# Two blocks in one kernel: the scale of the first norm made by matrix products, and a rope weight block whose rotated copy the host lays out

## The chip, the cores and the metric

The kernel runs on one core of one Trainium2 chip. The metric is the device time of one execution in microseconds; lower is better. TensorE (PE in the profile, PEld its weight loads), VectorE (DVE), ScalarE (ACT), GpSimd (POOL) and the DMA engines, whose work is issued by SyncE (SP), run side by side and wait for each other through semaphores.

## The reference

Two transformer blocks stand one after the other, each two layers deep, on 256 tokens of width 1024. Only the start of the first block is touched. Each layer makes six vectors from a condition `c` and scales and shifts a norm with two of them:

```
mod = silu(c) @ w_mod[l] + b_mod[l]                 # 1024 -> 6144
sh1, sc1, gt1, sh2, sc2, gt2 = split(mod, 6)
h = rms_norm(x, g_norm_mix[l]) * (1 + sc1) + sh1
proj = h @ w_in[l]                                  # 1024 -> 1952
q_d, k_d, v_d, cq, ckv, k_rope = split(proj)        # k_rope: the last 32 columns
```

`k_rope` is normed and rotated: with its two halves of 16 columns, rope gives (x1 cos - x2 sin, x2 cos + x1 sin). Two attentions (one dilated, one latent), an output product, a two-layer MLP and the residuals follow; then the second layer, and the second block (two other attentions, a dense MLP, a routed mixture of experts).

## The kernel before

All is float32. Each weight block of 1 MB (128 partitions x 2048 columns) is loaded into a tile `raw`, of which there are five (`NRAW`). ACT makes a rounded copy `whl` (hi), DVE the remainder (lo), and a product is three matmuls: hi by hi, hi by lo, lo by hi (`mm3`, `mtile`; a tile `mt` of 128 output rows takes 24 matmuls). The norm's factor over the tokens (`rstd`) is multiplied in after the product, when DVE takes a tile out of PSUM (`ev`); the scale over the features, `G = (1 + sc1) * g`, goes into `h_hi` and `h_lo` before it. So layer 0 can start no `mt` before `sc1` is there.

In layer 0 the scale comes from `mod_rows(0, ..., 8, 16, fine=14)`: PE spreads `silu(c)` over the partitions (`cb`), and for each of the eight groups of 128 outputs DVE multiplies a row block of the transposed weight by it and sums (`TENSOR_TENSOR_REDUCE`, in the profile CUSTOM_DVE_ANT_0 on `raw<-raw,cb`); the last 1 MB comes in two halves. The shift comes later and in another way, by `mod_part(0, 0, 8)`: per 1 MB block of the untransposed weight four matmuls of 512 columns (`mod<-raw,c_pad`), then a copy `mod_e` on DVE, four transposes `mod_t` on PE, a reduction and an addition on DVE. What the shift adds to the first four tiles (a bias for each output) is a small product `shb`; the later tiles have two more columns of h (256 to 258) that carry it.

The rope columns: for the rotation PE needs a tile of 64 columns, the 32 and the same with the halves exchanged. ACT and DVE make its hi and lo in three pieces each, out of a `raw` of 160 columns per k.

The order is not written by hand. Every instruction is recorded; `Sched` runs a list scheduler over the records with its own costs, and issues in the order that it finds. For each phase of the program the table `FINAL` gives a base order, three parameters of looking ahead, and the size and the seed of a noise on the priorities. `RESERVE` keeps buffers free for stretches of operation numbers. Every engine then runs its list strictly in that order. The whole of it is one source line, so the profile shows nearly all work at L641; tiles tell the work apart. The phase names are `start` (up to the rope tables), `first_mix0`, `first_mlp0`, and so on.

Of the kernel before, what the change touches and what calls it, by code (L numbers as in the profile page):

```python
# [159 lines left out]

class Op:
    __slots__ = ("i", "eng", "calls", "reads", "writes", "dur", "deps", "succ", "nd", "allocs", "start", "end", "prio",
                 "lat", "touch", "label", "phase", "after", "wait", "at", "hold", "goal")

    def __init__(self, eng):
        self.eng, self.calls, self.reads, self.writes, self.dur, self.lat = eng, [], [], [], 0.0, 0.0
# [19 lines left out]
class Sched:  # L186
# [2 lines left out]

    FINAL = {None: (1, (0.7, 0.2, 20), 0, 0),  # L190
             "start": (1, (0.3, 0.1, 10), 3, 377680),
             "first_mix0": (1, (0.6, 0.1, 30), 3, 220609),
             "first_mlp0": (1, (0.5, 0.1, 8), 8, 801976),
             "first_mix1": (1, (0.7, 0.3, 8), 15, 101696),
             "first_mlp1": (1, (0.5, 0.1, 30), 2, 868914),
             "second_mix0": (2, (0.6, 0.1, 20), 8, 40661),
# [1 line left out]
             "second_mix1": (1, (0.6, 0.1, 20), 10, 580917),  # L198
             "route": (2, (0.5, 0.1, 8), 0, 185731),
             "moe": (2, (0.3, 0.1, 10), 8, 572101)}  # L200
    RESERVE = {"t1": [(-73, 177)], "t2": [(247, 497), (1312, 1562), (2540, 2790), (2551, 2801), (3732, 3982), (3757, 4007), (3768, 4018), (3518, 4018), (1343, 1593), (3882, 4132)]}
    goal = None
    ISSUE = 1.22
    LATENCY = {("PE", "ACT"): 0.2, ("PE", "DVE"): 0.2, ("ACT", "PE"): 0.23, ("DVE", "PE"): 0.2, ("DVE", "ACT"): 0.13,
# [2 lines left out]
    def __init__(self, nc):  # L207
        self.nc = nc
        self.ops = []
        self.limits = {}  # L210
        self.group = None
        self.reserve = {}
        self.bufs = []
        self.bias = 0
        self.after = None
        self.phase = "start"
        self.gen = 0
        self.done_deps = -1
# [95 lines left out]
    def add(self, op):  # L314
        op.i = len(self.ops)
        op.phase = self.phase
        op.prio = op.i + self.bias
        op.after = self.after
        self.ops.append(op)
# [93 lines left out]
    def use(self, prios, plan):  # L413
        n = len(self.ops)
        noise = {}
        for op in self.ops:
            base, op.hold, amp, seed = plan.get(op.phase) or plan[None]
            op.prio = prios[base][op.i]
            if amp:
                if seed not in noise:  # L420
                    noise[seed] = np.random.RandomState(seed).rand(n)
                op.prio += amp * (noise[seed][op.i] - 0.5)

    def justify(self):

# [48 lines left out]
    def attempt(self):  # L474
# [23 lines left out]
        goal, last = self.goal, 0.0  # L498
# [14 lines left out]
        def can(op):  # L513
            need = {}
            op.allocs = [b for b in op.touch if id(b) not in allocated and b.ap is None]
            for b in op.allocs:
                k = (id(b.pool), b.tag)
                need[k] = need.get(k, 0) + 1
            for k, n in need.items():
                lim = self.limits[k]  # L520
                fr = lim - live[k]
                if fr < n:
                    self.short = k
                    return False

                p = pend[k]
                while ptr[k] < len(p) and id(p[ptr[k]]) in allocated:
                    ptr[k] += 1
                oldest = p[ptr[k]]
                if oldest in op.touch:  # L530
                    continue
                i = oldest.alloc_op.i
                r = self.LIMIT_RESERVE + sum(lo <= i <= hi for lo, hi in self.reserve.get(k, ()))
                if fr - n < max(min(r, lim - 1), lim == 1):
                    self.short = k
                    return False
            return True

        while left:
# [57 lines left out]
            if not ev:  # L597
                op = min((o for h in ready.values() for _, _, o in h), key=lambda o: o.i)
                assert not can(op)
                return self.short, op.i  # L600
            t = max(t, ev[0][0])
            while ev and ev[0][0] <= t + 1e-9:
                _, _, x = heapq.heappop(ev)
# [93 lines left out]
def small_arrays(I):  # L697
# [14 lines left out]
    for l in range(2):  # L712
# [22 lines left out]

BIG = ["w_kv_up", "w_router_2"]

PACKED = {"in_a": ("w_in", 0, 1024, 0, 1792, 8, 256), "in_b": ("w_in", 0, 1024, 1792, 160, 8, 160),
          "q_up": ("w_q_up", 0, 256, 0, 768, 2, 768), "out": ("w_out", 0, 1024, 0, 1024, 4, 512),
          "mlp_in": ("w_mlp_in", 0, 1024, 0, FF1, 8, 256), "mlp_out": ("w_mlp_out", 0, FF1, 0, 1024, 2, 1024),  # L740
          "mod": ("w_mod", 0, 1024, 0, 6144, 4, 512), "modT": ("w_modT", 0, 6144, 0, 1024, 2, 1024),
# [20 lines left out]
def body(ctx: ExitStack, tc: tile.TileContext, I, SN, out):  # L762
    nc = tc.nc
    S_ = Sched(nc)
# [395 lines left out]
    A.preload_act_table_set("natural_log_exp_and_others")  # L1160
    ca, cp = silu_c()
    mods = [tl("act", [128, 48], F32, f"mod{l}") for l in range(2)]
    mod_rows(0, c_rows("E4"), 8, 16, fine=14)

    trig = tl("cst", [128, 256], F32, "trig")
    trk = tl("cst", [64, 256], F32, "trk")
# [55 lines left out]
    def first_mix(l, acc, gt):  # L1222
# [55 lines left out]
        else:  # L1278
# [8 lines left out]
                        mm3(ps[j][:, :n], (w[0][:, k, sl], w[1][:, k, sl]), (h[kk][0][:, :n], h[kk][1][:, :n]), kk == 0, kk == 7)  # L1287
                        S_.end()
            ps.append(mtile(wsplit(rb[1][:, :, :128]), h))
        khl = hilo([128, 8, 64])  # L1290
        kr_src = rb[1][:, :, 128:160]
        for dsl, ssl in ((slice(0, 32), slice(0, 32)), (slice(32, 48), slice(16, 32)), (slice(48, 64), slice(0, 16))):
            split(kr_src[:, :, ssl], khl[0][:, :, dsl], khl[1][:, :, dsl])
        pr = mtile(khl, h, m=64, n=n)
        if l == 0:

            mod_part(0, 0, 8)
            shift_cols(h, shift(mods[0], 0))
            sp = t256("sh_pad").rearrange("p (k s) -> p k s", s=32)
            V.memset(sp, 0.0)  # L1300
            V.tensor_copy(sp[:, :, 0], mods[0][:, 0:8])
            pb = bank("shb")
            for hf in range(2):
                S_.begin()
                for o, r in ((0, rb[0]), (256, rb[1])):
                    for k in range(4):
                        T.matmul(pb[32 * k:32 * k + 32, o:o + r.shape[2]], sp[:, 4 * hf + k], r[:, 4 * hf + k],
                                 start=hf == 0 and o == 0, stop=hf == 1, skip_group_check=True)
                S_.end()
            e = t512("shb_e")  # L1310
            V.tensor_copy(e[:, :416], pb[:, :416])
            V.tensor_copy(e[:, 416:432], pb[:, 400:416])
            V.tensor_copy(e[:, 432:448], pb[:, 384:400])
            pt = bank("shb_t")
            S_.begin()
            for j in range(4):
                w = min(128, 448 - 128 * j)
                T.transpose(pt[:w, j * 128:(j + 1) * 128], e[:, j * 128:j * 128 + w], ident)
            S_.end()
            bc = tl("act", [128, 4], F32, "bc", "bc")  # L1320
            for m, c0, c1 in ((128, 0, 3), (64, 3, 4)):
                V.tensor_reduce(bc[:m, c0:c1], pt[:m, 128 * c0:128 * c1].rearrange("p (b r s) -> p b r s", r=4, s=32)[:, :, :, 0],
                                AX.X, OP.add)
            for j, pb in enumerate(ps + [pr]):
                early[id(pb)] = bc[:, j:j + 1]
            rope_tables()
            distances()
# [811 lines left out]
            run(S_.in_order)  # L2139


NRAW, NW, NT1, NR1, NT2 = 5, 6, 10, 7, 6
NAHEAD = 4
PM0 = 40
# [4 lines left out]
def host_arrays(I):  # L2149
# [5 lines left out]
    for n, (src, *how) in PACKED.items():  # L2155
        w = np.asarray(I["w_mod" if src == "w_modT" else src])
        w = w.transpose(0, 2, 1) if src == "w_modT" else w
        a[n] = pack(w.reshape(-1, *w.shape[-2:]), *how)
    gu = np.asarray(I["w_gu_exp_2"][0])
    g, u = gu[:, :, :FE], gu[:, :, FE:]  # L2160
    cols = [x[:, :, c:c + 256] for c in range(0, FE - 128, 256) for x in (g, u)] + [g[:, :, FE - 128:], u[:, :, FE - 128:]]
# [21 lines left out]
```

## Time and profile before

| what | value |
|---|---|
| time of the runs | 1593.61, 1597.28, 1599.37 us: median 1597.28 us |
| profiled execution | 1594.11 us, of which the span of the trace is 1592.3 us |
| PE busy | 1538.5 us, 97% of the span |
| DVE busy | 999.6 us, 63% |
| ACT busy | 797.7 us, 50% |
| moved by DMA | 384.35 MB, mean 241 GB/s |
| mean granted TensorE clock | 0.995 of full speed |

PE is busy nearly throughout, so what counts is the time in which it stands still or runs at half rate. The span is the time from the first to the last instruction; 1.81 us of the execution lie outside it.

### The profile page before, as it was taken

How to read it: one execution, taken by the hardware profiler on the slowest of the kernel's cores; microseconds unless marked ns; L12 is line 12 of the kernel's file. 1: busy time of each engine (PE TensorE's matmuls, PEld its weight loads, DVE VectorE, ACT ScalarE, POOL GpSimd, SP SyncE). 2: the span in 40 equal slices, each digit the busy share in tenths (PEclk: the TensorE clock that was granted, in tenths of full speed). 3: DMA queues.
4: the chain of work that ended last, by engine and by line, in shares of the span. 5: the costliest groups of instructions: out<-in, count | busy, mean ns of one | idle time of the engine just before them, and what ended most of it. 6: DMA issues, size and time to landing. Idle time of an engine off the chain costs nothing. (4 is left out here: it accounts for less than half of the span.)

```text
span 1592.3 us, 36673 instructions
## 1 busy us (share of the span) xinstructions
PE 1538.5 (97%) x15441; PEld 1356.7 (85%) x15441; DVE 999.6 (63%) x2117; ACT 797.7 (50%) x1519; POOL 9.9 (1%) x22
## 2 busy tenths in 40 slices
PE   5989999999999999999999999999999999998997
PEld 4777999998889999999999999999899755675564
DVE  7889898988998655788677666687856400000001
ACT  3857656567766655566865444466775200000000
POOL 0000000000000000010000000010000000000000
PEclk9999999999999999999999999999999999999999
DMA  9845598874146654554265555464337589999995
GB/s 350 314 183 212 203 358 334 331 279 171 42 159 223 227 189 159 185 186 137 91 225 180 191 202 195 163 212 143 123 117 307 210 354 414 418 417 392 418 418 220
DMA packets 59707, 384.35 MB, mean 241 GB/s; under 512 B 7936, under 2 KB 10640, under 8 KB 16912
## 3 DMA queue, kind: packets, MB, share of 16 engines
q1 hardware_dynamic: 57664, 379.78, 62.4%
q8 instruction: 125, 2.05, 0.5%
q0 software_dynamic: 832, 2.11, 0.5%
q14 instruction: 46, 0.38, 0.1%
q10 hardware_dynamic: 1040, 0.03, 0.0%
HBM read 380.83 MB, written 1.06 MB: 240 GB/s over the span
## 5 line engine op out<-in xcount | busy, mean ns | idle before, releaser
L641 PE MATMUL mt<-h_hi,whl 128*128 128x256 f32 (+2 forms) x3264 | 621.3, 285 | 11.4 <-ACT h_hi L641 11.4
L641 PEld LDWEIGHTS mt<-h_hi,whl 128*128 128x128 f32 (+1 forms) x3264 | 515.8, 189 | 25.6 <-ACT h_hi L641 11.9
L641 ACT ACTIVATE whl<-raw 128x1024 fp32r<-128x1024 f32 (+4 forms) x404 | 382.4, 960 | 282.3 <-PE mt L641 147.0
L641 DVE TENSOR_TENSOR whl<-raw,whl 128x1024 fp32r<-128x1024 f32 (+4 forms) x404 | 442.0, 1103 | 125.8 <-ACT whl L641 124.8
L641 PE MATMUL mt<-h_lo,whl 128*128 128x256 f32 (+2 forms) x1632 | 461.6, 283 | 1.0 <-DVE h_lo L641 1.0
L641 PEld LDWEIGHTS mt<-h_lo,whl 128*128 128x128 f32 (+1 forms) x1632 | 309.2, 189 | 1.6 <-DVE h_lo L641 1.4
L641 PE MATMUL acc<-a_hi,whl 128*128 128x256 f32 x1376 | 254.0, 280 | 0.0
L641 PEld LDWEIGHTS acc<-a_hi,whl 128*128 128x128 f32 x1376 | 216.4, 189 | 0.0
L641 PE MATMUL gu<-raw,xg 128*32 (+1 forms) x3520 | 201.8, 380 | 6.0 <-issue 6.0
L641 PE MATMUL acc<-a_lo,whl 128*128 128x256 f32 x688 | 192.6, 280 | 0.0
L641 PEld LDWEIGHTS gu<-raw,xg 128*32 128x32 f32 x3520 | 131.8, 110 | 70.4 <-issue 16.3
L641 DVE TENSOR_TENSOR sg<-sg,gu 128x512 f32<-128x512 f32 (+2 forms) x18 | 9.9, 561 | 205.0 <-PE gu L641 185.6
L641 PEld LDWEIGHTS acc<-a_lo,whl 128*128 128x128 f32 x688 | 129.3, 188 | 0.0
L641 PE MATMUL y<-raw,aT 128*32 (+1 forms) x1760 | 100.9, 384 | 4.9 <-DMA raw<-in_dn_e_dram 2.8
L641 DVE TENSOR_TENSOR ev<-mt,rstd 128x256 f32<-128x256 f32 (+1 forms) x166 | 69.4, 421 | 49.1 <-PE mt L641 48.5
L641 PEld LDWEIGHTS y<-raw,aT 128*32 128x32 f32 x1760 | 57.6, 111 | 43.9 <-issue 5.3
L641 DVE CUSTOM_DVE_ANT_0 raw<-raw,cb 128x1024 f32<-128x1024 f32 x64 | 76.9, 1221 | 5.4 <-ACT cb L641 3.0
L641 DVE SCALAR_TENSOR_TENSOR y_lo<-y,ws,y_hi 128x256 fp32r<-128x256 f32 x20 | 8.7, 480 | 100.3 <-ACT y_hi L641 100.3
L641 ACT ACTIVATE aT<-aT 128x256 f32<-128x256 f32 (+1 forms) x33 | 9.9, 346 | 104.1 <-PE aT L641 91.6
L641 ACT ACTIVATE y_hi<-y,ws 128x256 fp32r<-128x256 f32 x20 | 8.4, 471 | 105.8 <-issue 53.6
L641 ACT ACTIVATE sg<-gu 128x512 f32<-128x512 f32 (+2 forms) x18 | 8.7, 496 | 97.8 <-PE gu L641 97.8
L641 ACT ACTIVATE ev<-ev,bcol 128x256 f32<-128x256 f32 x64 | 32.0, 500 | 46.4 <-DVE bcol L641 31.4
(308 smaller groups left out, 1955.3 us busy)
## 6 DMA issues: line engine op xcount, KB each, us to landing
raw<-in_gu_e_dram SPq DMA_DIRECT2D x88, 1024.0 KB, 11.0
raw<-in_mlp_in_dram SPq DMA_DIRECT2D x32, 1024.0 KB, 5.1
raw<-in_mlp_out_dram SPq DMA_DIRECT2D x32, 1024.0 KB, 5.3
raw<-in_dn_e_dram SPq DMA_DIRECT2D x32, 1024.0 KB, 14.6
raw<-in_modT_dram SPq DMA_DIRECT2D x31, 1024.0 KB, 6.6
raw<-in_in_dram SPq DMA_DIRECT2D x24, 1024.0 KB, 4.8
raw<-in_gu_d_dram SPq DMA_DIRECT2D x22, 1024.0 KB, 4.9
raw<-in_mod_dram SPq DMA_DIRECT2D x16, 1024.0 KB, 7.1
```

The costliest lines, as they stand in the source:

```text
L641: getattr(real, m)(*[res(x) for x in a], **{k: res(x) for k, x in kw.items()})
```

## The change

Four things change.

1. `mod_rows(0, c_rows("E4"), 8, 16, fine=14)` becomes `mod_part(0, 8, 16)`: the scale is made as the shift is. The eight VectorE multiply-and-sum instructions and the spreading product `cb` go; 16 matmuls of 512 columns, a copy, four transposes, two reductions and the addition come. The weight is the untransposed one, in four blocks of 1 MB instead of three and two halves.
2. The host lays the block `in_b` out with 192 columns per k: 160 as before, then the two halves of the rope columns exchanged. The kernel splits columns 128 to 192 in one piece (one ACT, one DVE instruction, in each layer), and the copies of `shb_e` become one.
3. The noise is drawn by a number `ni` that is the operation's number plus a constant (`SH`), so that later phases draw what they drew before.
4. `FINAL` has other entries for `first_mix0` and `first_mlp0`, and `RESERVE` for `t2` is another list.

```diff
-                 "lat", "touch", "label", "phase", "after", "wait", "at", "hold", "goal")
+                 "lat", "ni", "touch", "label", "phase", "after", "wait", "at", "hold", "goal")
...
-             "first_mix0": (1, (0.6, 0.1, 30), 3, 220609),
-             "first_mlp0": (1, (0.5, 0.1, 8), 8, 801976),
+             "first_mix0": (1, (0.6, 0.1, 30), 3, 564062),
+             "first_mlp0": (2, (0.7, 0.3, 20), 1, 768677),
...
-        self.bias = 0
+        self.bias = self.shift = 0
...
+        op.ni = op.i + self.shift
...
-                    noise[seed] = np.random.RandomState(seed).rand(n)
-                op.prio += amp * (noise[seed][op.i] - 0.5)
+                    noise[seed] = np.random.RandomState(seed).rand(n + 1000)
+                op.prio += amp * (noise[seed][op.ni] - 0.5)
...
-    mod_rows(0, c_rows("E4"), 8, 16, fine=14)
+    mod_part(0, 8, 16)
...
-        khl = hilo([128, 8, 64])
-        kr_src = rb[1][:, :, 128:160]
-        for dsl, ssl in ((slice(0, 32), slice(0, 32)), (slice(32, 48), slice(16, 32)), (slice(48, 64), slice(0, 16))):
-            split(kr_src[:, :, ssl], khl[0][:, :, dsl], khl[1][:, :, dsl])
-        pr = mtile(khl, h, m=64, n=n)
+        pr = mtile(wsplit(rb[1][:, :, 128:192]), h, m=64, n=n)
+        S_.shift = SH[l]
...
-            V.tensor_copy(e[:, :416], pb[:, :416])
-            V.tensor_copy(e[:, 416:432], pb[:, 400:416])
-            V.tensor_copy(e[:, 432:448], pb[:, 384:400])
+            V.tensor_copy(e[:, :448], pb[:, :448])
...
+SH = (25, 29)
...
+    w = np.asarray(I["w_in"])
+    w = w[:, :, [*range(1792, 1952), *range(1936, 1952), *range(1920, 1936)]]
+    a["in_b"] = pack(w, 0, 1024, 0, 192, 8, 192)
```

The lists of the engines show what this moves. First VectorE, from the condition to the first of the norm's remainders `h_lo`. Before, where the ISA rows are the multiply-and-sum and the reading of its sum, and eight such pairs stand:

```order
L641 COPY c_pad<-c_act 128x8
L641 ISA raw,mod_140<-raw,cb 128x1024
L641 ISA mod_140 128x1
...
L641 TENSOR_TENSOR whl<-raw,whl 128x512
L641 TENSOR_TENSOR mod_140<-mod_140,SM 128x8
L641 SCALAR_TENSOR_TENSOR G_167<-mod_140,SM 128x8
L641 TENSOR_TENSOR whl<-raw,whl 128x512
L641 SCALAR_TENSOR_TENSOR h_lo<-x,G_167,h_hi 128x256 x6
```

And the same stretch of VectorE's list in the changed kernel:

```order
L642 COPY c_pad<-c_act 128x8
L642 COPY mod_e<-mod 128x512
L642 TENSOR_TENSOR whl<-raw,whl 128x512
L642 TENSOR_REDUCE mod_152<-mod_t 128x4 x2
L642 TENSOR_TENSOR whl<-raw,whl 128x512
L642 TENSOR_TENSOR mod_152<-mod_152,SM 128x8
L642 SCALAR_TENSOR_TENSOR G_161<-mod_152,SM 128x8
L642 TENSOR_REDUCE sqr<-sqs 128x256
L642 SCALAR_TENSOR_TENSOR h_lo<-x,G_161,h_hi 128x256 x5
```

Between the product and `G` two weight remainders `whl` now stand, where one stood, and behind `G` the sum of squares `sqr` has moved ahead of all `h_lo`. On ACT the square `sqs` of the first half of x and a third `whl` likewise stand ahead of the first `h_hi` now. On PE the product `ssq` over `sqr` stands ahead of the first `mt`; before, the 48 matmuls of the first two `mt` tiles stood ahead of it.

Second PE, around the last block of the shift's product and the rope tile (`mt` of 64 rows, 24 matmuls). Before:

```order
L641 MATMUL mt<-h_hi,whl 64x256
L641 MATMUL mod<-raw,c_pad 32x512 x4
L641 MATMUL mod_t<-K,mod_e 128x128 x4
L641 MATMUL shb<-raw,sh_pad 32x256 x4
L641 MATMUL shb<-raw,sh_pad 32x160 x4
...
L641 MATMUL mt<-h_hi,whl 128x258
```

And PE's list at this place in the changed kernel, where half of the rope tile stands behind the product:

```order
L642 MATMUL mod<-raw,c_pad 32x512 x4
L642 MATMUL mt<-h_hi,whl 64x256
L642 MATMUL mt<-h_lo,whl 64x256
...
L642 MATMUL mt<-h_hi,whl 64x256
L642 MATMUL mod_t<-K,mod_e 128x128 x4
L642 MATMUL shb<-raw,sh_pad 32x256 x4
L642 MATMUL shb<-raw,sh_pad 32x192 x4
```

The transposes `mod_t`, which need VectorE's copy `mod_e`, stood right behind the product; now 12 matmuls of the rope tile stand between.

Third VectorE, in the attention of layer 0, where the latent query's tiles (`qm`) are multiplied (`qm_g`) and the keys are scaled (`km`). Before:

```order
L641 SCALAR_TENSOR_TENSOR rn_hl<-rn_hi,K,rs_r 128x256
L641 TENSOR_TENSOR whl<-raw,whl 128x1024
L641 TENSOR_TENSOR ev<-mt,rstd 128x256
L641 TENSOR_TENSOR km<-rnb,kn_g 64x256 x2
L641 TENSOR_TENSOR whl<-raw,whl 128x1024 x2
L641 TENSOR_TENSOR qm_g<-qm,trq 128x512
L641 COPY bcol<-mt 128x1
L641 TENSOR_TENSOR km<-rnb,kn_g 64x256 x3
```

And VectorE's list in the changed kernel, where its first `qm_g` stands:

```order
L642 SCALAR_TENSOR_TENSOR rn_hl<-rn_hi,K,rs_r 128x256
L642 TENSOR_TENSOR whl<-raw,whl 128x1024
L642 TENSOR_TENSOR qm_g<-qm,trq 128x512
L642 TENSOR_TENSOR km<-rnb,kn_g 64x256 x3
L642 SCALAR_TENSOR_TENSOR rs_l<-hss,rs_l 128x256
L642 SCALAR_TENSOR_TENSOR rs_r<-rs_l,rs_r 128x256
L642 TENSOR_TENSOR km<-rnb,kn_g 64x256
```

One weight remainder of 1024 columns stands ahead of this `qm_g`, where three stood behind the same `rn_hl` before. From the second layer on the lists differ in single places only.

## Rows read from the trace of the kernel before

**Rows 1.** Waits of PE in the first 200 us: total, times, longest
```profile
PE mt L641 <- ACT h_hi L641: 11.4, 1, 11.4
...
PE hss L641 <- DVE bcol L641: 3.5, 1, 3.5
PE mod_t L641 <- DVE mod_e L641: 1.2, 1, 1.2
```

**Rows 2.** Timeline of the start: start us, us, engine, operation, count, idle before
```profile
8.58 1.23 DVE L641 CUSTOM_DVE_ANT_0 raw<-raw,cb 128x1024 f32<-128x1024 f32 x1 [3.04 <-ACT cb L641]
...
14.48 0.38 SPq L641 DMA_DIRECT2D x<-in_xT_dram  x1
...
17.89 0.63 ACT L641 ACTIVATE whl<-raw 128x512 fp32r<-128x512 f32 x1 [1.38 <-DMA raw<-in_in_a_dram]
...
18.55 0.17 DVE L641 SCALAR_TENSOR_TENSOR G<-mod,SM 128x8 f32<-128x8 f32 x1
18.63 0.69 DVE L641 TENSOR_TENSOR whl<-raw,whl 128x512 fp32r<-128x512 f32 x1
18.75 2.51 ACT L641 ACTIVATE h_hi<-x,G 128x256 fp32r<-128x256 f32 x6 [0.23 <-DVE G L641]
...
19.31 0.58 PE L641 MATMUL mt<-h_hi,whl 128*128 128x256 f32 x1 [11.40 <-ACT h_hi L641]
...
23.00 1.05 ACT L641 ACTIVATE sqs<-x 128x1024 f32<-128x1024 f32 x1
...
24.08 2.07 DVE L641 TENSOR_REDUCE sqr<-sqs 128x256 f32<-128x1024 f32 x1 [0.18 <-ACT sqs L641]
...
27.14 0.60 PE L641 MATMUL ssq<-sqr,K 128*128 128x256 f32 x2
```

**Rows 3.** Waits of the DMA queue's issuer, first 110 us
```profile
SPq L641 <- DMA raw<-in_modT_dram: 7.2, 5, 2.4
```

**Rows 4.** Timeline at the shift's product
```profile
37.30 1.06 PE L641 MATMUL mod<-raw,c_pad 128*32 128x512 f32 x8
37.41 0.42 DVE L641 TENSOR_TENSOR ev<-mt,rstd 64x256 f32<-64x256 f32 x1 [3.10 <-PE mt L641]
...
39.53 0.66 PE L641 MATMUL mod_t<-K,mod_e 128*128 128x128 f32 x4 [1.16 <-DVE mod_e L641]
...
40.92 0.18 DVE L641 COPY sh_pad<-mod 128x8 f32<-128x8 f32 x1
...
41.20 1.61 PE L641 MATMUL shb<-raw,sh_pad 128*32 128x256 f32 x32 [1.01 <-issue]
...
42.74 0.39 PE L641 MATMUL mt<-h_hi,whl 128*128 128x258 f32 x1
```

**Rows 5.** Timeline at PE's longest wait after the start
```profile
83.46 2.36 DVE L641 TENSOR_TENSOR whl<-raw,whl 128x1024 fp32r<-128x1024 f32 x2
85.83 0.69 DVE L641 TENSOR_TENSOR qm_g<-qm,trq 128x512 f32<-128x512 f32 x1
...
86.56 0.66 ACT L641 ACTIVATE hsq<-qm 128x256 f32<-128x256 f32 x2 [3.40 <-DVE qm_g L641]
86.73 1.59 PE L641 MATMUL hss<-hsq,K 128*32 128x256 f32 x8 [3.52 <-DVE bcol L641]
```

**Rows 6.** Stretches: busy (count) PE, PEld, DVE, ACT, POOL; granted clock; DMA share; GB/s
```profile
21.00:23.40 2.40, 2.40 (x13) 2.40 (x12) 2.37 (x5) 2.40 (x6) 0.00 (x0) 1.00 1.03 425
23.40:27.00 3.60, 3.60 (x32) 3.60 (x31) 3.42 (x4) 3.25 (x6) 0.00 (x0) 1.00 1.02 419
...
86.70:88.20 1.50, 1.47 (x8) 0.58 (x8) 1.46 (x4) 0.90 (x3) 0.00 (x0) 0.50 1.01 426
88.20:91.50 3.30, 3.30 (x16) 3.24 (x16) 2.33 (x5) 1.89 (x5) 0.00 (x0) 0.50 0.99 407
91.50:97.00 5.50, 5.50 (x47) 5.26 (x46) 3.94 (x10) 0.12 (x1) 0.00 (x0) 0.98 0.40 140
...
200.00:300.00 100.00, 100.00 (x846) 100.00 (x845) 90.74 (x164) 58.87 (x91) 0.00 (x0) 1.00 0.90 338
```

More of the change, by code (lines that the diff above doesn't have):

```diff
@@ L200 @@
              "moe": (2, (0.3, 0.1, 10), 8, 572101)}
-    RESERVE = {"t1": [(-73, 177)], "t2": [(247, 497), (1312, 1562), (2540, 2790), (2551, 2801), (3732, 3982), (3757, 4007), (3768, 4018), (3518, 4018), (1343, 1593), (3882, 4132)]}
+    RESERVE = {"t1": [(-73, 177)], "t2": [(1312, 1562), (1343, 1593), (1346, 1596), (2540, 2790), (2551, 2801), (3732, 3982), (3757, 4007), (3767, 4017), (3768, 4018)]}
     goal = None
@@ L531, in can @@
                     continue
-                i = oldest.alloc_op.i
+                i = oldest.alloc_op.ni
                 r = self.LIMIT_RESERVE + sum(lo <= i <= hi for lo, hi in self.reserve.get(k, ()))
@@ L599, in attempt @@
                 assert not can(op)
-                return self.short, op.i
+                return self.short, op.ni
             t = max(t, ev[0][0])
@@ L736 @@
 BIG = ["w_kv_up", "w_router_2"]
-PACKED = {"in_a": ("w_in", 0, 1024, 0, 1792, 8, 256), "in_b": ("w_in", 0, 1024, 1792, 160, 8, 160),
-          "q_up": ("w_q_up", 0, 256, 0, 768, 2, 768), "out": ("w_out", 0, 1024, 0, 1024, 4, 512),
+PACKED = {"in_a": ("w_in", 0, 1024, 0, 1792, 8, 256), "q_up": ("w_q_up", 0, 256, 0, 768, 2, 768), "out": ("w_out", 0, 1024, 0, 1024, 4, 512),
           "mlp_in": ("w_mlp_in", 0, 1024, 0, FF1, 8, 256), "mlp_out": ("w_mlp_out", 0, FF1, 0, 1024, 2, 1024),
```

## The prediction

> **What bounds the kernel now.** I read the waits of PE first, because PE is busy for 97% of the span and only its standing still or running at half rate can be won. In the first 200 us they are few [rows 1]: 11.4 us before the first product over h, 3.5 us before a small product `hss` in the attention, 1.2 us before the transposes `mod_t`. The change is made exactly there, at the start of layer 0, so I read the timeline of the start next [rows 2]. The reader is to see a chain: VectorE multiplies and sums from 8.58 us on, the gain `G` is made at 18.55, ACT makes the first `h_hi` from 18.75, and PE begins at 19.31. Then the timeline at the shift's product [rows 4], since it shows in this very kernel what the new way of making the scale costs, and the one at the 3.5 us wait [rows 5], which a new order may remove. Last, stretches with the granted clock [rows 6].
>
> **Is VectorE or the DMA what the start waits for?** The issuer SP waits five times for a block of the scale's weight to land, 7.2 us together [rows 3], and the last such wait ends with the issue at 14.48 us [rows 2]. I read this as the landing of the last half block. `G` comes 4.07 us later. So of the 18.55 us, 14.5 are DMA, which the change leaves as long as it is (four blocks of 1 MB either way), and only 4 us are VectorE's backlog.
>
> **The new chain to G.** The shift's product shows the price: its last block starts on PE at 37.30 and `sh_pad`, which needs the finished sum, starts at 40.92, 3.62 us later [rows 4]. From 14.48 this gives 18.1 us. But VectorE's list has the second remainder `whl` ahead of the addition. Its hi copy starts on ACT at 17.89, when its data lands, and ends at 18.52; the remainder takes 0.69 us, to 19.2; the addition and `G` take 0.2 us each [rows 2]. So `G` is there at about 19.6 us, 1 us later than now. The bounds: 18.3 us if that data lands early enough to put no wait into the chain, 20.7 us if product and transposes run at half rate (1.06 + 0.66 us more [rows 4], and the remainder behind them).
>
> **What stands behind G.** Now the sum of squares `sqr`, 2.07 us, comes ahead of `h_lo` on VectorE, and `ssq`, 0.60 us, ahead of the first `mt` on PE [rows 2]. Its input `sqs` (1.05 us on ACT [rows 2], behind the copy that ends at 18.52) is there at 19.6 and delays nothing more. 19.6 + 2.07 + 0.60 and 0.1 for handing over is 22.4 us for the first `mt`, against 19.31: **3.1 us later** (bounds 1.8 and 4.2 from those of `G`). Queued behind `sqr` on VectorE are eight `h_lo`; PE takes 24 matmuls on four of them, so they do not bind.
>
> **What is given back.** `ssq` is not made a second time between the `mt`: 0.6 us. Half of the rope tile, 12 matmuls, covers the copy `mod_e`, and so the 1.2 us wait of `mod_t` [rows 1, 4] goes. On the other side `rstd` comes only after the second `ssq`, which now stands just ahead of the rope tile, so that three `ev` of 0.42 us [rows 4], made before while VectorE had nothing else (it stood idle 3.10 us before the last `ev`), now lie among the steps that lead to `sh_pad`, `shb` and the weight remainders: 1.2 us. Late by 3.1 - 0.6 - 1.2 + 1.2 = **2.5 us** when the ordinary tiles run (before, from 42.74 us [rows 4]). Bounds 0.0 (the early `G`, and the `ev` hidden) and 3.6.
>
> **The clock at the start.** The first matmuls over h run at half rate: 13 in 2.40 us, then 32 in 3.60 us [rows 6], though the column of the clock says 1.00 there. PE now works on the scale's four blocks before, but then stands idle from about 17 us to `ssq` at 21.7. After the 3.5 us wait of `hss` the granted clock was 0.50 for 4.8 us [rows 1, 6], so I take the half rate again and no gain. The Trainium skill ("TensorE: Matmul & The Clock Gate", Part 1) says that the throttled state is the default and that activity releases it; read alone it would promise that the new matmuls warm the array for the first `mt`. By it the sum would be 2.0 us lower; the row after a wait speaks against it.
>
> **The other edits.** One split of the rope columns for three, in each of two layers, saves ACT and VectorE some tenths, while PE has other tiles to run; bare it would be worth less than 0.7 us a layer, one such remainder [rows 2]. The 32 more columns of `in_b` are 0.13 MB a layer, 0.3 us at the 425 GB/s of a full stretch [rows 6], hidden because PE does not wait for that block. The new order of `first_mlp0` can win nothing: PE is busy for all of 200 to 300 us [rows 6]; it could lose what a new wait costs, 1 us as the `mod_t` wait. Both edits at nothing, with 1 us to either side.
>
> **The new order in the attention.** The 3.5 us wait has a clear cause [rows 5]: two remainders of together 2.36 us stand ahead of `qm_g` on VectorE, ACT's squares `hsq` of `qm` start when `qm_g` ends, and `hss` on PE stands ahead of 36 ready matmuls. The price is the wait of 3.5 us and the half clock after it: 1.5 us and 3.3 us at 0.50 [rows 6], of which half, 2.4 us, is lost. Together 5.9 us. In the new list one remainder stands ahead of the first `qm_g`, and the products of the second group of queries come only after three pieces of ordinary work (two products over scores and 24 matmuls). I take 5.5 us as won, leaving 0.4 for a short wait. The bounds are 0 (the wait moves) and 5.9.
>
> **The sum.** +2.5 - 5.5 = -3.0 us. The profiled execution took 1594.11 us, so 1591.1 there; it lies 3.17 us under the median of the runs, and against that median, 1597.28, the sum gives **1594.3 us**. Differences within 0.3% (4.8 us) count as no change.
>
> **Rivals.**
> - *Forecast:* later start, attention wait gone, 1594.3 us (its own range 1590 to 1598). Chance 0.46.
> - *The array stays fast and the scale comes as soon as the chain allows.* PE's new work before the first `mt` lets it start at full rate; half of the 4.1 us from 19.31 to 23.4 [rows 2, 6] is won, 2.0 us: -5.0 us, 1592.3 us. For it: the four blocks follow each other up to the end of the product. Against it: the idle time before `ssq`. Chance 0.22. With the early `G` it would come to -6.3.
> - *VectorE falls behind (slower).* VectorE is at work almost throughout around the tiles, and what it lost at the start it carries on: every remainder `whl` is late, the `hss` wait stays because its squares again wait behind remainders, and three more remainders of 1.2 us (half of 2.36 [rows 5]) become PE's wait: +2.5 + 3.5 = +6.0 us, 1603.3 us. It decides as soon as two remainders stand ahead of what PE's next product needs. Chance 0.15.
> - *The gain moves.* The same wait with its half clock comes back at another product of the attention, less what is lost at the start already by standing there: between 0 and +2.5 us, 1597 to 1600 us. For it: the order comes from a list scheduler whose costs are not those of the trace (all such waits are between engines that the list kept apart). Chance 0.17.
>
> **Numbers.** The range takes in the rival with the fast array and its early `G`, with some 3 us of spread between runs (1593.61 to 1599.37), and leaves out most of the slower rival: 1586 to 1601 us. Faster by over 0.3% means under 1592.5: a third of the forecast's cases and three quarters of the fast array's, 0.32. Slower by over 0.3% means above 1602.1: most of the slower rival, and a little of the others, 0.15. The rest, 0.53, is no change.
>
> **What would show it.** The first `mt` at 21.1 to 23.5 us with `ssq` ahead of it, and `G` at 18.3 to 20.7; no wait of `mod_t` over 0.3 us; `shb` and the first `mt` of 258 columns later by 1 to 3 us; no wait over 1 us and no stretch at 0.50 between 78 and 95 us; PE's list past 105 us about 3 us ahead of before. Wrong is the forecast if `sqr` runs before `G` is there, if PE starts the `mt` at full rate, or if a wait of some us stands at a later `hss`, `S` or `PT` of the attention.

## The result, and the profile after

The changed kernel took 1604.76 us (median of 6 runs, 1603.61 to 1607.87), the kernel before 1596.74 us beside it. The ratio is 1.0057 with a 95% interval of 1.0047 to 1.0067: slower by 0.57%; the medians lie 8.0 us apart. The forecast of 1594.3 us and its range up to 1601 were wrong.

The profiled execution after took 1607.34 us, its span 1605.3. It is 13.2 us over the one of before, more than the medians differ: it is the second slowest of the six runs after (1603.61 to 1607.87), and the 1594.11 us of before lie near the lowest run of that kernel (1593.61). 3.0 us of the 13.2 arise behind the first product of the experts alone (table below); I read the trace up to there.

The start, by the timeline of the kernel after (start us, us, engine, operation, count, idle before):

```profile
14.93 1.94 PE L642 MATMUL mod<-raw,c_pad 128*32 128x512 f32 x8 [0.58 <-DMA raw<-in_mod_dram]
...
17.68 1.11 PE L642 MATMUL mod_t<-K,mod_e 128*128 128x128 f32 x4 [0.81 <-DVE mod_e L642]
...
19.80 0.17 DVE L642 SCALAR_TENSOR_TENSOR G<-mod,SM 128x8 f32<-128x8 f32 x1
...
20.08 1.92 DVE L642 TENSOR_REDUCE sqr<-sqs 128x256 f32<-128x1024 f32 x1
...
22.06 1.22 PE L642 MATMUL ssq<-sqr,K 128*128 128x256 f32 x2 [3.26 <-DVE sqr L642]
22.72 0.78 PE L642 MATMUL mt<-h_hi,whl 128*128 128x256 f32 x1
...
25.43 0.62 PE L642 MATMUL mt<-h_hi,whl 128*128 128x256 f32 x2
25.85 0.31 PE L642 MATMUL mt<-h_lo,whl 128*128 128x256 f32 x1
...
42.66 1.72 PE L642 MATMUL shb<-raw,sh_pad 128*32 128x256 f32 x32 [1.22 <-issue]
44.31 0.38 PE L642 MATMUL mt<-h_hi,whl 128*128 128x258 f32 x1
```

The reader is to see the chain of the forecast: `G` at 19.80, `sqr` and `ssq` ahead of the first `mt`, which comes at 22.72 instead of 19.31 [rows 2] and at half rate (0.62 us for a pair, 0.40 from 26.0 us on) until 25.8. At `shb` and the first `mt` of 258 columns 1.5 and 1.6 us of the 3.4 are left [rows 4].

The waits of PE in the first 250 us of the kernel after (total, times, longest):

```profile
PE mod L642 <- DMA raw<-in_mod_dram: 9.1, 4, 7.5
PE ssq L642 <- DVE sqr L642: 4.1, 2, 3.3
PE mt L642 <- DVE qm L642: 2.4, 1, 2.4
...
PE mt L642 <- DVE whl L642: 0.8, 1, 0.8
...
PE mod_t L642 <- DVE qm_g L642: 0.5, 1, 0.5
PE S L642 <- DVE bcol L642: 0.5, 1, 0.5
```

The 3.5 us of `hss` [rows 1] are gone. In their place stand three waits a few us later, 3.4 us together (for `qm`, `qm_g` and `bcol`). VectorE's timeline there, then PE's, and the stretch with its granted clock (busy and count of PE, PEld, DVE, ACT, POOL; clock; DMA share; GB/s):

```profile
88.28 1.21 DVE L642 TENSOR_TENSOR whl<-raw,whl 128x1024 fp32r<-128x1024 f32 x1
...
89.82 1.21 DVE L642 TENSOR_TENSOR whl<-raw,whl 128x1024 fp32r<-128x1024 f32 x1
90.95 0.68 DVE L642 TENSOR_TENSOR qm_g<-qm,trq 128x512 f32<-128x512 f32 x1
91.55 1.21 DVE L642 TENSOR_TENSOR whl<-raw,whl 128x1024 fp32r<-128x1024 f32 x1
...
93.90 0.67 DVE L642 TENSOR_TENSOR qm<-qm_g,rnb 128x512 f32<-128x512 f32 x1
...
94.71 0.55 PE L642 MATMUL mt<-h_hi,whl 128*128 128x258 f32 x1 [2.38 <-DVE qm L642]
```

```profile
80.00:100.00 20.00, 16.28 (x108) 11.96 (x106) 17.76 (x37) 7.96 (x15) 0.00 (x0) 0.91 0.84 326
```

It is the picture of [rows 5] once more, at another product: remainders `whl` of later tiles stand ahead of what PE's next product waits for. Of 20 us PE is busy for 16.28, at a mean clock of 0.91. The same stretch of the kernel before:

```profile
80.00:100.00 20.00, 16.01 (x107) 13.34 (x106) 16.90 (x36) 8.81 (x22) 0.00 (x0) 0.83 0.68 252
```

Where the rest of the loss arises shows a ladder: how much later than in the kernel before, in us, the same product starts in each profiled execution (in the columns `acc last` and `y last`: ends). `wo` is the projection behind the first attention, `acc` the MLP's second product (its first and its last matmul in layer 0, its first in layer 1), `gu` the first product of the experts, `y` their last.

```
                             mt first  wo first  acc first  acc last  acc layer 1  gu first  y last
before (us)                     19.31    138.03     182.65    353.69       491.83   1249.65  1581.63
after                            +3.4      +1.8       +2.7      +6.1         +9.3     +10.2    +13.2
after_old_mlp0                   +3.6      +3.8       +3.9      +4.0         +7.7      +8.7     +9.2
after_old_both                   +2.6      +3.1       +3.2      +6.5        +10.2     +11.2    +12.3
before_new_mlp0                  -0.0      +2.6       +3.1      +3.7         +3.7      +3.8     +4.9
layout_only                      +0.0     +25.9      +26.0     +25.9        +26.4     +26.4    +28.6
change_old_order                 +0.3      +0.7       +0.7      +0.7         +0.8      +1.0     +2.1
layout_old_order                 -0.1      +2.6       +2.6      +4.0         +4.2      +4.2     +3.9
scale_old_order                  -0.3      +1.1       +1.0      +0.9         +1.0      +1.1     +4.0
new_order_first_mix_only         +3.5      +3.1       +4.0      +3.9         +3.9      +5.6     +6.4
before_whl_later                 -0.3      -1.0       -1.0      -1.2         -1.1      -1.3     -2.7
after_whl_later                  +3.2      +1.4       +2.3      +9.0        +10.6     +11.5    +13.5
after_sqr_later                  +1.3      +1.4       +2.2      +4.2         +5.9      +6.8    +10.0
change_old_order_whl_later       +0.2      -2.4       -2.4      -2.5         -2.4      -2.4     -4.6
```

After the change the lag is 1.8 us behind the first attention, near the 1.6 us at 44 us. It then grows by 3.4 us inside the first MLP and by 3.2 more up to the MLP of layer 1, in stages of which the change touches nothing but the order and one split. The order differs there in more than the single places that the section on the change speaks of: between 400 and 450 us of the kernel before, in the attention of layer 1, some 70 of VectorE's 152 instructions stand elsewhere in the changed kernel's list.

The waits of PE show where these 6.6 us go. From the first to the last `acc` of the MLP the kernel before has none, the one after has 2.3 us (1.0, 0.8 and 0.5); the granted clock is 1.00 in both from 98 us to beyond that stage. From there to the `acc` of layer 1 the waits are 3.1 us before and 6.1 after. The longest of them, before and then after:

```profile
PE ssq L641 <- DVE sqr L641: 1.5, 2, 0.8
PE rnb L641 <- DVE bcol L641: 0.8, 1, 0.8
```

```profile
PE ssq L642 <- DVE sqr L642: 2.7, 3, 1.6
PE mt L642 <- DVE mn L642: 1.5, 1, 1.5
PE PT L642 <- ACT PTs L642: 0.7, 1, 0.7
PE PT L642 <- ACT vd L642: 0.5, 1, 0.5
```

### The profile page after: what moved, and what is told of

Read it like the earlier page. It is cut to its first block, busy times and chain, and to the rows that moved or that the text cites. A ratio compares the mean times of both kernels' runs of the same rounds, so it can differ in the third digit from the quotient of the medians.

```text
span 1605.3 us, 36685 instructions
## 1 busy us (share of the span) xinstructions
PE 1545.9 (96%) x15461; PEld 1359.9 (85%) x15461; DVE 991.1 (62%) x2090; ACT 794.8 (50%) x1513; POOL 9.9 (1%) x22
## 3 DMA queue, kind: packets, MB, share of 16 engines
HBM read 381.09 MB, written 1.06 MB: 238 GB/s over the span
## 5 line engine op out<-in xcount | busy, mean ns | idle before, releaser
L642 ACT ACTIVATE whl<-raw 128x1024 fp32r<-128x1024 f32 (+3 forms) x400 | 382.6, 968 | 312.5 <-PE mt L642 160.6
L642 DVE TENSOR_TENSOR whl<-raw,whl 128x1024 fp32r<-128x1024 f32 (+3 forms) x400 | 440.7, 1112 | 137.3 <-ACT whl L642 136.1
L642 PEld LDWEIGHTS y<-raw,aT 128*32 128x32 f32 x1760 | 64.3, 112 | 41.0 <-issue 7.3
L642 DVE CUSTOM_DVE_ANT_0 raw<-raw,cb 128x1024 f32<-128x1024 f32 x56 | 67.1, 1219 | 0.5 <-ACT cb L642 0.5
```

Of the source, the lines that this page charges most:

```text
L642: getattr(real, m)(*[res(x) for x in a], **{k: res(x) for k, x in kw.items()})
```

## Experiments

All were timed beside the kernel before; a ratio is to it, with its 95% interval. Together, with the change itself first:

```
after                        1604.76 us   1.0057 (1.0047 to 1.0067)
after_old_mlp0               1603.97      1.0043 (1.0026 to 1.0060)
after_old_both               1606.03      1.0059 (1.0042 to 1.0076)
before_new_mlp0              1599.45      1.0017 (1.0005 to 1.0029)
layout_only                  1623.16      1.0161 (1.0141 to 1.0181)
change_old_order             1598.56      1.0015 (1.0003 to 1.0027)
before_whl_later             1593.94      0.9986 (0.9975 to 0.9997)
after_whl_later              1601.90      1.0037 (1.0023 to 1.0051)
after_sqr_later              1604.03      1.0045 (1.0030 to 1.0060)
new_order_first_mix_only     1599.83      1.0028 (1.0017 to 1.0040)
change_old_order_whl_later   1596.16      1.0004 (0.9994 to 1.0014)
layout_old_order             1597.15      1.0007 (0.9994 to 1.0020)
scale_old_order              1597.79      1.0006 (0.9993 to 1.0018)
```

### First theory: the new order of the first MLP

The MLP is where the lag grew, and the change gives its phase a new entry in the planner's table. So the first runs put entries back, or put the new one into the kernel before.

after_old_mlp0, the changed kernel with one old entry:

```diff
-             "first_mlp0": (2, (0.7, 0.3, 20), 1, 768677),
+             "first_mlp0": (1, (0.5, 0.1, 8), 8, 801976),
```

> The changed kernel with the planner's entry for first_mlp0 as it was in the kernel before; all else as changed. Theory O (the new order inside first_mlp0 is what costs most): the changed kernel lags 2.7 us at the first product of the MLP's second half and 8.7 us at the norm after it, so some 6 us come back: 1604.8 - 6 = about 1599 (1597 to 1601), the three modulation rows on VectorE in the last 25 us of the MLP are gone, and its end lags by 2 to 3 us only. Rival L (the order is innocent; the start's lateness meets a full VectorE and grows by itself): no change, 1603 to 1606, and the lag still grows inside the MLP.

Measured: 1603.97 us, which the runs don't tell from the change's 1604.76. The mechanism was half right: the MLP adds 0.1 us now instead of 3.4. But the attention of layer 1, whose entry nobody touched, adds 3.7 us (+4.0 to +7.7). Theory O, that this one order costs 6 us, falls.

after_old_both puts the entry of `first_mix0` back too:

```diff
-             "first_mix0": (1, (0.6, 0.1, 30), 3, 564062),
+             "first_mix0": (1, (0.6, 0.1, 30), 3, 220609),
```

> The changed kernel with both old entries, for first_mix0 and first_mlp0: the change of the code alone. Theory O: about 1599 to 1602; the start stays 2.5 to 3.4 us late, and the attention of the first layer either has its old stall of 3.5 us for hss or one like it, so the lag at the end of first_mix0 is +2 to +5 and does not grow after. Rival L: 1603 to 1606. Rival N (each order fits only the code that it was found for, so an old entry with new code is worse): 1606 or more.

Measured: 1606.03 us, where rival N begins, and not to be told from the change's 1604.76. Theory O falls here too. With the MLP's old entry in both runs, the MLP adds 0.1 us in the one and 3.3 in the other. An entry does not name an order: it says how priorities are disturbed, and the order that comes out depends on all that was planned ahead of it.

before_new_mlp0 is the converse, the kernel before with the new entry for `first_mlp0` alone:

```diff
-             "first_mlp0": (1, (0.5, 0.1, 8), 8, 801976),
+             "first_mlp0": (2, (0.7, 0.3, 20), 1, 768677),
```

> The kernel before with only the new entry for first_mlp0: no operation is added or removed. Theory O: 1596.7 + 6 = about 1603 (1601 to 1605), with modulation rows left on VectorE at the end of the MLP. Rival L: 1595 to 1598, since nothing is late ahead of the MLP.

Measured: 1599.45 us, between both theories. Its MLP adds 0.6 us (+3.1 to +3.7); the 2.6 us ahead of it arise in the start, in an order that is that of before: they are differences of the granted clock (see the last section).

layout_only takes the scale back to VectorE and leaves the rope layout, both entries old, the list of reserved buffers as in the changed kernel:

```diff
-    mod_part(0, 8, 16)
+    mod_rows(0, c_rows("E4"), 8, 16, fine=14)
...
-SH = (25, 29)
+SH = (6, 10)
```

> Only the rope columns laid out side by side by the host; the scale of the first norm is made on VectorE as before, and both entries of the planner are the old ones. My working: six small splits a layer become two, all in time in which VectorE is not waited for: 1596.7 +- 1.5, first product at 19.3 us as before. Rival R (removing work moves the planner's order, and the removal or the larger packed block costs elsewhere): 1599 or more, or 1594 or less.

Measured: 1623.16 us, 27 us lost where I expected none, 26 of them ahead of `wo`. Its stretch from 80 to 100 us and the waits of PE there:

```profile
80.00:100.00 20.00, 11.09 (x77) 5.26 (x76) 19.32 (x51) 13.39 (x31) 0.00 (x0) 0.85 0.99 379
```

```profile
PE rnb L642 <- DVE rn_hl L642: 6.9, 3, 4.7
```

VectorE is at work for 19.32 of the 20 us, and PE, idle for 9 of them, waits for one of its small pieces. That made the order itself the suspect, for the change too.

### Second theory: the order, not the code

To take the order out of the comparison, the next kernels don't plan: each emits a written list of operations.

```diff
+    def kept(self):
+        self.schedule()
+        ops = {o.i: o for o in self.order}
+        self.again([ops[i] for i in ORDER])
...
-    run(S_.schedule)
+    run(S_.kept)
```

`again` only gives each buffer out at its first use in the new list. ORDER is the list of the kernel before, without what the change removes, and with the four products, the copy, the transposes and the reductions of the scale where VectorE's rows stood.

> The changed kernel emitted in the order of the kernel before: every instruction that both have stands where it stood, the four products, the copy, the transposes and the two reductions of the scale stand where VectorE's rows stood, and only what the change removes is missing. Theory P (the code costs little, the new orders that the planner found for it cost the 8 us): the first product comes at 20.0 to 20.8 us instead of 19.3, the lag is below 1.5 us at every later stage, the old stall of 3.5 us before hss stands where it was, and the time is 1596.7 + 0 to 1.5, about 1597. Rival C (the code itself costs, whatever the order): 1601 or more, with a lag that grows in the first layer.

Measured: 1598.56 us, ratio 1.0015. The timeline of its start, and a line of the waits of PE in its first 250 us:

```profile
12.38 1.56 PE L654 MATMUL mod<-raw,c_pad 128*32 128x512 f32 x8 [0.54 <-DMA raw<-in_mod_dram]
...
14.89 1.06 PE L654 MATMUL mod<-raw,c_pad 128*32 128x512 f32 x8 [0.95 <-DMA raw<-in_mod_dram]
...
18.85 0.17 DVE L654 SCALAR_TENSOR_TENSOR G<-mod,SM 128x8 f32<-128x8 f32 x1
...
19.61 0.58 PE L654 MATMUL mt<-h_hi,whl 128*128 128x256 f32 x1 [1.76 <-ACT h_hi L654]
```

```profile
PE hss L654 <- DVE bcol L654: 3.5, 1, 3.5
```

The first product is 0.3 us late, the stall of `hss` is back where it was, and the lag never exceeds 1.0 us before the experts. Rival C, the code, is out: of 0.57% the code carries 0.15% (0.03 to 0.27). That is 2.4 us against the runs beside it, 0.9 more than theory P allowed.

The two parts of the change alone, in the same order. First the layout, with layout_only's `mod_rows` for the scale:

```diff
-    mod_part(0, 8, 16)
+    mod_rows(0, c_rows("E4"), 8, 16, fine=14)
```

> Only the rope columns laid out side by side, as in the run that took 1623 us, but emitted in the order of the kernel before with the removed splits and copies left out. Theory P (that run's 27 us are its order, not the layout): 1596.2 +- 1.2, and every landmark within 1 us. Rival C (the larger packed block and the 64 more columns of the shift's product cost by themselves): 1600 or more.

Then the scale, with the rope columns split as before:

```diff
-        pr = mtile(wsplit(rb[1][:, :, 128:192]), h, m=64, n=n)
+        khl = hilo([128, 8, 64])
...
+        pr = mtile(khl, h, m=64, n=n)
```

> Only the scale of the first norm made on TensorE, in the order of the kernel before; the rope columns are split as before. Theory P: first product at 19.5 to 20 us, lag of 0.2 to 1 us throughout, 1596 to 1599. With the run of the layout alone it says which part carries the 2.35 us that the change costs in the old order: 1598 to 1599 if it is the scale, 1596 to 1597 if it is the layout or a chance of the runs. Rival C (half-rate products of the scale delay the start by 2 us or more even in the old order): first product after 21 us and 1599 or more.

Measured: 1597.15 and 1597.79 us; neither ratio (1.0007, 1.0006) can be told from 1. The layout that took 27 us in an order of its own takes about 1 us in the old one, 3 at most by its interval. Which part carries the 0.15% stays open; together they make it up.

new_order_first_mix_only has the changed kernel's own order for its first 735 operations, up to the end of the first mixing layer, and the old order from there:

```
ORDER = new[:735] + [i for i in old if i not in new[:735]]     # how its list is put together; the kernel holds the finished list
```

> The changed kernel in its own order through the whole first mixing layer (735 instructions), and from there on in the order of the kernel before. Theory D (the loss has two parts: the new order of the first layer costs 2 to 3 us, that of the MLP and the second layer another 6): lag of 2.3 to 3 us at the MLP's first product and no more than 3.5 us after it, 1598.5 to 1600.5. Rival E (a first layer that ends late makes any MLP late, whatever its order, since the weights are fetched later): the lag grows to 6 us or more inside the MLP or the norm after it, 1602 to 1605.

Measured: 1599.83 us, ratio 1.0028, the time of theory D. The lag is 4.0 us at the MLP, 1 us over what theory D said, and 3.9 us behind it: a late first layer doesn't make the MLP late (rival E is out). So, from ratios that were each taken against the kernel before, the 0.57% divide into 0.15% code, 0.13% order of the first layer, 0.29% order from the MLP on. By the intervals of the ratios the last is good to about 0.15 and clear of noise; the 0.13% is good to about 0.17, so by the times alone it can't be told from nothing. Whether the parts simply add is assumed: the reverse, the old order first and the new one from the MLP on, was not tried.

### Single instructions moved

These kernels keep the planner's order, but for two or three operations that are moved behind another one, here in the kernel before:

```diff
+MOVE = ((490, 348), (513, 490))
...
+        for i, at in MOVE:
+            op = next(o for o in order if o.i == i)
+            order.remove(op)
+            order.insert(next(n for n, o in enumerate(order) if o.i == at) + 1, op)
...
-    run(S_.schedule)
+    run(S_.moved)
```

> The kernel before, in its own order but for two instructions: the two weight remainders on VectorE (83.5 to 85.8 us) ahead of the product with the rope table for which hss waits go behind the next small norm. Nothing is added or removed. Theory W (these two and nothing else make the stall of 3.5 us and the half clock after it): hss comes 2.4 us earlier, the stretch at half the clock is shorter or gone, 1596.7 - 2.4 to - 5.9, about 1593. Rival M (the wait only moves, since VectorE has the same work between 80 and 100 us): 1595.5 to 1598, with a new wait of 2 us or more within the next 15 us.

Measured: 1593.94 us, ratio 0.9986 (0.9975 to 0.9997), the fastest of all and faster than both kernels. The timeline with VectorE's rows and `hss`, then the stretch:

```profile
85.11 0.69 DVE L657 TENSOR_TENSOR qm_g<-qm,trq 128x512 f32<-128x512 f32 x1
...
86.01 1.15 PE L657 MATMUL hss<-hsq,K 128*32 128x256 f32 x8 [1.12 <-DVE bcol L657]
...
89.54 2.35 DVE L657 TENSOR_TENSOR whl<-raw,whl 128x1024 fp32r<-128x1024 f32 x2
```

```profile
80.00:100.00 20.00, 17.21 (x127) 14.05 (x124) 19.46 (x44) 10.91 (x26) 0.00 (x0) 1.00 0.71 264
```

The two remainders, 2.36 us ahead of `qm_g` in [rows 5], now stand at 89.54. The wait falls from 3.52 to 1.12 us and the half clock after it is gone (1.00 for 0.83). That is 2.4 us from each, the second as the prediction priced it; but a new wait of 1.1 us for a small norm (`rnb`) comes at 92.8. Of the 3.7 us that this leaves, the trace shows 2.8 (a lag of +1.6 us at the scores at 77 us, of -1.2 at those at 95 us), the runs 2.3. That is just short of theory W's lower end of 2.4 us, and outside rival M's times.

change_old_order_whl_later does the same in the change with the old order, by its list (the two remainders have the numbers 465 and 488 in it; these are pieces of the list):

```diff
-395, 281, 282, 465, 536, 488, 313, 316
+395, 281, 282, 536, 313, 316
...
-322, 540, 323, 287, 324
+322, 540, 323, 465, 488, 287, 324
```

> The change in the order of the kernel before, and in it the two weight remainders of VectorE behind the small norm. If the two effects add: change in the old order + 2.35, remainders later - 2.3 against the kernel before, so 1596.2 + 0, from 1595 to 1597.5, with no wait over 1.5 us and no half clock between 80 and 100 us. If the change has already taken the time that the remainders give back: 1598 to 1599.

Measured: 1596.16 us, ratio 1.0004: the two effects add, and the change then can't be told from the kernel before; it is 2 to 3 us slower than the same move without the change.

after_whl_later moves the three remainders seen above (88.28, 89.82, 91.55) in the changed kernel:

```diff
+MOVE = ((465, 618), (488, 465), (525, 488))
```

> The changed kernel in its own order but for three instructions: the weight remainders on VectorE at 88.3, 89.8 and 91.6 us go behind the row minima that follow. Theory W: the waits of 0.5, 0.5 and 2.4 us up to the product at 94.7 us and the half clock to 97.6 us go, 1604.8 - 3 to - 5, about 1601. Rival M (the wait only moves): 1603.5 to 1606, with a new wait before 110 us.

Measured: 1601.90 us. The waits of PE from 80 to 110 us:

```profile
PE S L658 <- DVE mod L658: 2.1, 1, 2.1
PE mt L658 <- DVE qm L658: 0.5, 1, 0.5
```

The trace shows rival M: the wait of 2.4 us falls to 0.5, a wait of 2.1 us that was not there comes at the next scores, and the lag at `wo` falls from 1.8 to 1.4 us only. The times speak for theory W: the runs are some 3 us under those of the change (0.20% by the ratios, good to about 0.17). But the profiled execution, of 1607.57 us, is the slowest of its ten runs, so its trace need not show what the others gained, and I don't decide it.

after_sqr_later moves the first sum of squares and its product behind the first tiles' `h_lo` and matmuls:

```diff
+MOVE = ((50, 48), (51, 84))
```

> The changed kernel in its own order but for two instructions: the first sum of squares on VectorE (2.07 us) goes behind the last of the first eight h_lo, and its product ssq on TensorE behind the first 17 groups of the first tiles. Theory S (step a of the forecast: the sum of squares is what delays the first product): first product at 20.2 to 20.8 us instead of 22.7, and 0.5 to 2.5 us of it are left at 65 us: 1604.8 - 0.5 to - 2.5, about 1603. Rival V (VectorE is the bound up to 65 us, the same work in another order ends at the same time): the first product is earlier all the same, but the lag at 65 us and the time do not change, 1604 to 1606.

Measured: 1604.03 us, not to be told from 1604.76. The first product comes 2.1 us earlier:

```profile
20.57 0.58 PE L658 MATMUL mt<-h_hi,whl 128*128 128x256 f32 x1 [2.92 <-ACT h_hi L658]
```

Of that 0.7 us are left at a product `vm` at 69 us (68.70 for 69.44), the lower end of theory S, and 0.4 us at `wo`. The sum of squares is what delayed the first product, as theory S has it; that it mattered for the time isn't shown, and 1604.03 us lies in rival V's times.

## Why the prediction was wrong

**The start was read rightly.** `G` was forecast for 19.6 us and came at 19.80, the first `mt` for 22.4 and came at 22.72, at half rate, as [rows 6] said against the page of the Trainium skill that the forecast weighed. There was some luck in `G`: the last block's product ran at half rate (1.94 us for the 1.06 of [rows 4]), so that the sum was there some 1 us after the 18.1 us taken for it; but the remainder ahead of the addition ended later still, as it did in the forecast. Moving the sum of squares gave 2.1 of the 3.4 us back, as that step had it. The 2.5 us forecast for the ordinary tiles were 1.6 at their first product, inside the bounds of 0 to 3.6.

**The step "I take 5.5 us as won" failed.** The `hss` wait went, and the lag at `wo` is still 1.8 us, against 1.6 us at 44 us: the attention gave nothing back. I had looked in the new list at what stands ahead of the first `qm_g`, and not at the next group, where three remainders stand ahead of `qm_g` and `qm`. The rival "the gain moves" describes it; its 1597 to 1600 us are what new_order_first_mix_only measured, 1599.83. Moving the remainders in the kernel before shows how little of such a wait is there to win: 2.3 of 5.9 us. I had bounded the gain by the wait and its half clock without asking what VectorE is late with next. The sign "no wait over 1 us and no stretch at 0.50 between 78 and 95 us" failed with the 2.38 us wait that ends at 94.71 and the granted clock of 0.50 from 94.7 to 97.6 us.

**The step "it could lose what a new wait costs, 1 us" failed by more.** For the new order behind the first layer I had a ceiling from PE being busy in [rows 6], and took one small wait for the floor. By the ratios above that order costs 0.29%, 4.6 us (2 to 7), by the profiled execution 6.6 us, of which 5.3 are longer waits of PE: 2.3 in the MLP and 3.0 more in the stage up to the `acc` of layer 1. For that second stage the prediction had no term at all, since the lists were said to differ in single places only from there on. That PE has no idle time in the old order limits what a new order can win, and says nothing on what it can lose. The first MLP of the kernel after shows one way, VectorE's rows and PE's near its end:

```profile
351.97 1.22 DVE L642 CUSTOM_DVE_ANT_0 raw<-raw,cb 128x1024 f32<-128x1024 f32 x1
...
353.11 0.42 DVE L642 TENSOR_TENSOR ev<-mt,rstd 128x256 f32<-128x256 f32 x1
...
354.64 0.38 PE L642 MATMUL acc<-a_hi,whl 128*128 128x256 f32 x1 [1.00 <-ACT a_hi L642]
...
357.76 1.22 DVE L642 CUSTOM_DVE_ANT_0 raw<-raw,cb 128x1024 f32<-128x1024 f32 x1
```

Rows of the next layer's modulation, 1.22 us each, have been left for the last 8 us, and one stands ahead of the `ev` for which ACT's `a_hi` and PE wait (1.00 us, and 0.5 more for `a_lo`). In the kernel before the last such row begins 20.7 us before the MLP's last matmul (353.69):

```profile
L641 DVE CUSTOM_DVE_ANT_0 raw<-raw,cb x3: 1220/1222/1227, 326.8 to 333.0; 128x1024 f32<-128x1024 f32 x3
```

This cause is argued from the rows, not tested by a run, and it isn't the only way: in after_old_both and layout_old_order, without such a row there, the same two products wait 1.3 and 1.1 us behind remainders `whl`. The size varies: the same new order took 174.5, 177.7 and 173.0 us from first to last `acc` in three executions (after, after_whl_later, after_sqr_later), while the old order took 170.8 to 171.0 us in six of seven, and once 172.5 (layout_old_order). PE's waits in that stretch are 2.3, 2.9 and 1.4 us in the three. In after_whl_later a stretch at half clock follows a wait of 1.8 us, which costs some 3.4 us more:

```profile
228.10:234.90 6.80, 6.27 (x28) 5.97 (x29) 5.44 (x8) 5.79 (x9) 0.00 (x0) 0.50 1.01 420
```

Why the waits differ between executions of one order stays open. The rival *VectorE falls behind* forecast 1603.3 us, near the 1604.76 measured, but by another path: the `hss` wait, on which it put 3.5 us, was gone, and half of the loss or more came behind the first mixing layer. That its number is near is luck; its condition, two remainders ahead of what PE's next product needs, did hold at 88 to 94 us.

**The other edits** were rightly priced near nothing, but only in the old order: the layout alone took 0.07% there, 1.1 us, which can't be told from nothing, and all of the code 0.15%, 2.4 us.

## What to carry to other kernels

When a planner with a noise on its priorities makes the order, an edit is two changes: emit the new code in the old order first, and the code's own price shows (here 0.15% of 0.57%; for the layout alone 0.07%, not told from nothing, of 1.61%). A stall that is gone from its place has been won only when the next products behind it start earlier; look in the new list at what the waited-for engine does ahead of each of the next few, not of the first alone. Two instructions moved by hand on an engine that isn't the bound gave 2.3 us; no exchange of table entries in these runs gave a gain clear of noise.

## What the runs showed of the hardware

The same instructions after the same wait get different clocks in different executions. Before `shb` PE waits 1.0 us in every kernel with the old start. In change_old_order the 32 matmuls of `shb` then take 1.72 us (1.61 in the kernel before [rows 4], with fewer columns); in layout_old_order, with the same matmuls in the same order there, 2.88 us, and the stretch from 42 to 46 us has a granted clock of 0.57. First its row and this stretch, then the same stretch of change_old_order, with 1.00:

```profile
41.98 2.88 PE L654 MATMUL shb<-raw,sh_pad 128*32 128x256 f32 x32 [1.01 <-PE mod_t L654]
```

```profile
42.00:46.00 4.00, 4.00 (x38) 2.86 (x39) 3.71 (x11) 3.28 (x5) 0.00 (x0) 0.57 0.92 329
```

```profile
42.00:46.00 4.00, 4.00 (x51) 3.54 (x43) 4.00 (x12) 3.63 (x6) 0.00 (x0) 1.00 0.88 333
```

scale_old_order has 0.73 there, before_whl_later 0.63, and before_new_mlp0 0.61, though its list up to 130 us is that of the kernel before, which has 1.00. The half rate of the first `mt` varies as well: a pair takes 0.63 us until 23.4 us in the kernel before, until 25.3 in layout_old_order and until 25.9 in before_new_mlp0. The two together make nearly all of the lag of 2.6 us that layout_old_order and before_new_mlp0 have at `wo`: it is -0.1 and -0.0 us at the first product, and +2.3 and +2.4 us at 49 us, at the first product `css` of the mixing layer. So a ladder from one execution is good to some 2 us, in the MLP of after_whl_later to some 3, and even a lag that arises within a stage says something only where its granted clock is looked at. The products of the scale, too, took 1.94 us each, all four, in the kernel after, but 1.56 and 1.06 us for the last two in change_old_order, and so end 0.9 us earlier there. (`G` comes 0.95 us earlier, but there only one remainder stands ahead of it, not two.) The Trainium skill ("TensorE: Matmul & The Clock Gate", Part 1) says that the point at which matmuls that begin at half rate change to the full one differs from run to run; the pairs of `mt` and the products of the scale agree. Of a fall after a wait of 1 us, in some executions only, that sentence says nothing.
